# A two-layer diffusion trunk on one core: VectorE takes over GpSimd's parts of h^T and of weights around the ends of sublayers

## The chip, the core and the metric

The kernel runs on one core of one Trainium2 chip, as one launch. The time is the device time of that launch in microseconds, as the median of several runs. The core has five engines that run their own instruction streams in order and meet through semaphores: TensorE (PE, matrix products and transposes), VectorE (DVE), ScalarE (ACT), GpSimd (POOL) and SyncE (SP, which here issues most transfers).

## The reference: what is computed

640 tokens of width 1024 (128 context tokens, then 512 latent ones) go through two layers of three sublayers each: an FFN, a mixer, an FFN. Each sublayer is

```python
h = rms_norm(x, g_norm[i, 0]) * (1.0 + scale) + shift
y, aux = fn(h)
return x + weight * gate * rms_norm(y, g_norm[i, 1]), aux
```

where `shift`, `scale` and `gate` come from a product of the conditioning with `w_mod`, one set for context and one for latent tokens. `fn` is a SwiGLU of inner width 2816 (sublayers s = 0, 2, 3, 5), gated linear attention (GLA) with 4 heads and two scan directions (s = 1), or multi-head latent attention with 16 heads (s = 4). In GLA, q, k, v, an output gate r and a low-rank z are projections of h; the logarithm of the decay is `log_sigmoid(z @ w_gate + b_gate) / 16` for each head and direction; the scan in chunks of 64 tokens yields o, which is normalised, gated by silu(r) and multiplied with `w_out`. All is float32.

## The kernel before

**Tiles and precision.** The tokens are five tiles of 128, in two groups: g = 0 is tiles 0 to 2, g = 1 tiles 3 and 4. h is kept transposed (h^T, eight blocks of 128 features). To keep float32's accuracy with TensorE's faster format, each operand is split into a rounded high part (hi) and the remainder (lo), and each product is three matmuls (`mm3`, L116 to L118: hi by hi, hi by lo, lo by hi). So every weight and every h^T needs a cast on ScalarE (L109, L418, L1054) and a subtraction (L111, L419, L1055) on VectorE or GpSimd. Which of the two takes a weight's lo part is a list, `self.lo`, that rotates with each `split`: it is GpSimd alone during GLA's heads, and GpSimd and VectorE in turn in some of the output projections.

**A sublayer's end.** `sweep` multiplies the inner result with the output weights, tile by tile, and `chain` then takes each tile t through the end of the sublayer and the start of the next: the sum of squares of y on ScalarE (L139), the factors of the norm on VectorE (L126 to L134), the product with the gate (L440), the sum with x (L443), the norm of the new x, the normalisation (L447), eight transposes on TensorE (L406), and the scale and shift as eight activations (L417) into `hraw`, followed by hi (L418) and lo (L419). A store of x goes out on GpSimd's queue (L444). The chain of g = 0 runs beside the products of g = 1. `sum_rows` adds a later modulation row on VectorE during four of the sweeps.

**An FFN's start.** The first two of 22 columns of blocks, f = 0 and 1, are ordinary products. The others use a scheme with seven products of half size instead of eight: `mix` builds three differences of quarters of h^T (`tt`, tiles t1, t2, t3, each hi and lo), and `mixed_weights` four sums of quarters of a weight block (L591 to L594) for each unit u, of which there are 20. For s = 2, 3 and 5 `mix` is called in `chain`, in two pieces: columns 0 to 191 of each half after tile 3, and 192 to 319 after tile 4; its lo parts are GpSimd's. The weights come through three buffers (`raw`), so a load waits until the tile three before it is split.

**GLA.** `gla` loads tables, makes z and the gate weights wg, then for head 0 q and k (`gla_qk`), the logarithms (`gla_log`, `gla_log_end`), their sums (`gla_decay`) and v (`gla_v`). Then for each head h: the weights of head h + 1 are loaded and split, `gla_head` does the scan of head h in seven levels (L1022 to L1033: differences, an exponential, a product with q and k, five matmuls, a masked copy), and the projections and logarithms of head h + 1 follow.

**Order.** The code is written without an explicit order; a scheduler puts it into one stream per engine by priorities that follow the order of the program text and by its own estimates of durations, and within an engine the order is then fixed. `later` gives a part a later priority.

## Time and profile before

| | us |
|---|---|
| median of 3 runs | 2798.01 |
| lowest, highest | 2792.17, 2800.95 |
| the profiled execution | 2802.07 |
| its span in the profile | 2800.3 |

All durations below come from the profiled execution, whose own time is 1.8 us over its span and 4.1 over the median. Its page gives the share of each engine: TensorE 96% of the span, VectorE 68%, ScalarE and GpSimd 48% each, and a mean granted TensorE clock of 0.984. The stages by time: the first FFN to about 505, GLA to about 888, the FFNs of s = 2 and 3 to about 1352 and 1820, latent attention to about 2353, the last FFN to the end. In rows of the timeline the first number is the start, the second the busy time; xN counts instructions in one row, and the bracket at the end gives the idle time of the engine just before the row and what ended it. In the rows of stretches, the counts of instructions stand in brackets behind each engine's busy time. Line numbers are those of the kernel before.

### The profile page before, as it was taken

To read this page: it belongs to the slowest core of one execution; us is meant where nothing else is said; L and a number is where in the kernel's file an instruction comes from. 1 tells how busy PE (TensorE), PEld (TensorE's weight loads), DVE (VectorE), ACT (ScalarE), POOL (GpSimd) and SP (SyncE) were. 2 spreads that over 40 slices of the span, in tenths; PEclk is the share of its full clock that TensorE was granted. 3 is DMA by queue.
4 is the path that set the end of the run, shared out by engine and by line. 5 is a ranking of instruction groups with operands and counts; after the bars stand their busy time and mean duration, and the time that the engine had idled before them with its cause. 6 is when DMAs were issued, how large, how long until landed. Compare 5 with 4: busy or idle time off the path is not lost.

```text
span 2800.3 us, 43895 instructions
## 1 busy us (share of the span) xinstructions
PE 2698.8 (96%) x16670; PEld 2445.7 (87%) x16670; DVE 1896.2 (68%) x2499; ACT 1357.5 (48%) x2460; POOL 1344.8 (48%) x1093
## 2 busy tenths in 40 slices
PE   6999999899998999999999999999999998999998
PEld 5999987788877899987899998789999887999987
DVE  6777666577746767667776756677666677777636
ACT  3544426545546544425544433565555536445423
POOL 2555455343224555555456555404333367556534
PEclk9999999999999999999999999999999999999999
DMA  8444556311225344467344455641111285222445
GB/s 240 145 152 163 183 197 225 115 53 50 65 89 174 106 143 144 158 205 253 124 130 136 132 179 203 208 125 42 47 41 62 77 266 180 69 90 91 165 142 186
DMA packets 227378, 389.03 MB, mean 139 GB/s; under 512 B 17096, under 2 KB 160752, under 8 KB 227168
## 3 DMA queue, kind: packets, MB, share of 16 engines
q1 hardware_dynamic: 217968, 364.16, 40.2%
q0 software_dynamic: 5264, 19.24, 1.8%
q10 hardware_dynamic: 3936, 2.84, 0.4%
q8 instruction: 131, 2.15, 0.3%
q14 instruction: 79, 0.65, 0.1%
HBM read 356.00 MB, written 30.18 MB: 138 GB/s over the span
## 4 chain that ended last, share of the span: by engine, by line
PE 84%; DVE 7%; ACT 2%; DMA 2%; issue 2%; POOL 1%; SPq 0%; ACTq 0%; DVEq 0%; POOLq 0%
PE p L117 9%; PE p L116 9%; PE p L118 9%; PE x L116 7%; PE x L118 7%; PE x L117 7%; PE z L116 3%; PE z L117 3%; PE z L118 3%; PE m L305 2%; PE q L116 2%; PE q L117 2%; PE q L118 2%; PE j L116 2%; PE t L118 2%
## 5 line engine op out<-in xcount | busy, mean ns | idle before, releaser
L109 ACT CAST whi<-raw 128x1024 fp32r<-128x1024 f32 (+1 forms) x288 | 300.0, 1044 | 478.3 <-PE p L118 278.6
L111 DVE TENSOR_TENSOR wlo<-raw,whi 128x1024 fp32r<-128x1024 f32 (+1 forms) x248 | 340.6, 1381 | 262.5 <-ACT whi L109 259.5
L116 PE MATMUL p<-whi,t1h 128*128 128x512 f32 x1040 | 410.6, 395 | 1.9 <-POOL t1h L524 1.2
L118 PE MATMUL p<-whi,t1l 128*128 128x512 f32 x1040 | 408.4, 393 | 1.3 <-POOL t1l L525 1.3
L117 PE MATMUL p<-wlo,t1h 128*128 128x512 f32 x1040 | 408.3, 393 | 0.0
L1055 DVE TENSOR_TENSOR wlo<-raw,whi 128x512 fp32r<-128x512 f32 (+2 forms) x273 | 295.5, 1093 | 132.4 <-ACT whi L1054 131.3
L1055 DVE TENSOR_TENSOR wlo<-s,whi 128x512 fp32r<-128x512 f32 x320 | 280.1, 885 | 91.1 <-PE m L305 51.3
L591 POOL TENSOR_TENSOR s<-raw,raw 128x512 f32<-128x512 f32 x80 | 108.1, 1351 | 441.5 <-DMA raw<-in_w_ffn_in_dram 343.6
L1054 ACT CAST whi<-raw 128x512 fp32r<-128x512 f32 (+2 forms) x273 | 165.3, 610 | 164.3 <-PE q L117 72.0
L1054 ACT CAST whi<-s 128x512 fp32r<-128x512 f32 x320 | 194.3, 618 | 97.1 <-PE z L117 50.0
L116 PEld LDWEIGHTS p<-whi,t1h 128*128 128x128 f32 x1040 | 196.7, 189 | 45.4 <-issue 3.0
L118 PEld LDWEIGHTS p<-whi,t1l 128*128 128x128 f32 x1040 | 196.6, 189 | 43.9 <-POOL t1l L525 2.2
L117 PEld LDWEIGHTS p<-wlo,t1h 128*128 128x128 f32 x1040 | 196.8, 189 | 40.8 <-issue 0.2
L1316 POOL TENSOR_SCALAR p<-p,st 128x640 f32<-128x640 f32 (+1 forms) x68 | 119.9, 1763 | 203.4 <-DVE st L1315 187.8
L116 PE MATMUL x<-hh,whi 128*128 128x320 f32 x640 | 204.1, 319 | 3.5 <-DVE aT L628 3.5
L524 POOL TENSOR_SCALAR t1h<-aT 128x384 fp32r<-128x384 f32 (+1 forms) x128 | 91.9, 719 | 228.5 <-PE p L117 189.0
L118 PE MATMUL x<-hh,wlo 128*128 128x320 f32 x640 | 197.7, 309 | 0.0
L117 PE MATMUL x<-hl,whi 128*128 128x320 f32 x640 | 197.5, 309 | 0.0
L111 POOL TENSOR_TENSOR wlo<-raw,whi 128x1024 fp32r<-128x1024 f32 x40 | 107.2, 2690 | 160.4 <-ACT whi L109 158.7
L525 POOL TENSOR_TENSOR t1l<-aT,t1h 128x384 fp32r<-128x384 f32 (+1 forms) x128 | 143.5, 1122 | 10.0
L116 PEld LDWEIGHTS x<-hh,whi 128*128 128x128 f32 x640 | 120.0, 188 | 28.4 <-issue 24.3
L592 POOL TENSOR_TENSOR s<-s,raw 128x512 f32<-128x512 f32 x80 | 133.7, 1671 | 0.2
(427 smaller groups left out, 7968.0 us busy)
## 6 DMA issues: line engine op xcount, KB each, us to landing
raw<-in_w_ffn_out_dram SPq DMA_DIRECT2D x176, 512.0 KB
raw<-in_w_ffn_in_dram SPq DMA_DIRECT2D x160, 512.0 KB
wm<-in_w_mod_dram SPq DMA_DIRECT2D x112, 512.0 KB
raw<-in_w_mod_dram SPq DMA_DIRECT2D x32, 512.0 KB
raw<-in_mla_w_out_dram SPq DMA_DIRECT2D x32, 512.0 KB
xd<-x POOLq DMA_DIRECT2D x25, 512.0 KB, 3.7
x<-xd SPq DMA_DIRECT2D x25, 512.0 KB
raw<-in_w_ffn_in_dram SPq DMA_DIRECT2D x32, 256.0 KB
```

What stands on the lines that cost most here:

```text
L109: nc.scalar.copy(hi[:, :n], src[:, :n])
L111: (self.lo[0]).tensor_tensor(lo[:, :n], src[:, :n], hi[:, :n].bitcast(F32), op=ALU.subtract)
L116: mm(out, lh, rh, start=start, stop=False, **kw)
L117: mm(out, lh, rl, start=False, stop=False, **kw)
L118: mm(out, ll, rh, start=False, stop=stop, **kw)
L524: self.nc.gpsimd.tensor_scalar(ah, a, 1.0, 0.0, op0=ALU.mult, op1=ALU.add)
L525: self.nc.gpsimd.tensor_tensor(al, a, ah.bitcast(F32), op=ALU.subtract)
L591: G(s1, w21, w22, op=ALU.add)
L592: G(s2, s1, w11, op=ALU.subtract)
L1054: self.nc.scalar.copy(hi, src)
L1055: (engine or self.nc.vector).tensor_tensor(lo, src, hi.bitcast(F32), op=ALU.subtract)
L1316: (nc.gpsimd if h < MH - 1 else V).tensor_scalar(pp, pp, ri, None, op0=ALU.mult)
```

## The change

What it does, in five parts:

1. `sum_rows` issues the small loads and memsets of a row (`mod_gains`) ahead of its first load of weights, and `sweep` takes this first step at its start.
2. The lo part of h^T is always VectorE's (`gentle` is gone), and the mix of h^T is made in one piece after tile 4, with all its operations on VectorE and each difference split as soon as it is there.
3. The sums for unit 0's weights are VectorE's in the FFNs of s = 2, 3 and 5; the other units' sums stay GpSimd's.
4. All of GLA's lo parts (head weights, wg, output projection) are VectorE's.
5. In GLA, z's weights get two tiles of the pool `room` instead of the common weight buffers; wg is split after z's first product; v of the first group comes before z's second product; the masks are loaded by SP, later; and each head's logarithms are made one head earlier.

```diff
 def sum_rows(self, ps):
         for p in ps:
             o = (p % 9) * D
+            b = self.mod_gains(p)
+            yield
             acc = [...]
...
-                if kc == 0:
-                    b = self.mod_gains(p)
 def to_hT(...):
-        (nc.gpsimd if gentle else nc.vector).tensor_tensor(
-            hT[1][:, :, c : c + P], h, hT[0][:, :, c : c + P].bitcast(F32), op=ALU.subtract
-        )
+        nc.vector.tensor_tensor(hT[1][:, :, c : c + P], h, hT[0][:, :, c : c + P].bitcast(F32), op=ALU.subtract)
 def chain(...):
-                self.to_hT(u, hT, t, g, pt, cols=cols[:, :, cond, :], raw=raw, gentle=s == 2 and g == 0)
-                if ffn and t > 2:
-                    self.mix(slice(0, 4), *((0, 192), (192, HT))[t - 3], nc.gpsimd)
+                self.to_hT(u, hT, t, g, pt, cols=cols[:, :, cond, :], raw=raw)
+        if g and s in (2, 3, 5):
+            self.mix(slice(0, 4), 0, HT)
 def sweep(...):
+        next(steps, None)
-    def mix(self, ks, a, b, engine=None):
+    def mix(self, ks, a, b):
+        split = lambda t, src: self.hi_lo(t[0][:, ks, a:b], t[1][:, ks, a:b], src)
         V.tensor_tensor(h11, h12, h11, op=sub)
+        split(self.tt[0], h11)
         V.tensor_tensor(h12, h22, h12, op=sub)
         V.tensor_tensor(h22, h22, h11, op=sub)
+        split(self.tt[1], h22)
         V.tensor_tensor(h21, h21, h22, op=sub)
-        for t, src in zip(self.tt, (h11, h22, h12)):
-            self.hi_lo(t[0][:, ks, a:b], t[1][:, ks, a:b], src, engine)
+        split(self.tt[2], h12)
 def mixed_weights(..., engine):
-        G = nc.gpsimd.tensor_tensor
+        G = engine.tensor_tensor
 def ffn(...):
-            W[u] = self.mixed_weights(w_in, u % 2, f)
+            W[u] = self.mixed_weights(w_in, u % 2, f, nc.gpsimd if u or s == 0 else V)
 def gla(...):
-            mf = self.scratch(896).rearrange("p (l i) -> p l i", i=P)
-            nc.scalar.dma_start(mf, I["masks"])
-            nc.vector.tensor_copy(masks, mf)
-            nc.vector.tensor_scalar(diag2, self.ident, 2.0, None, op0=ALU.mult)
-            wz = [self.wp.tile([P, 1024], F32R, tag=x, ...) for x in ("whi", "wlo")]
+            wz = [T_([P, 1280], "room", F32R, bufs=7)[...] for _ in range(2)]
...
-            nc.scalar.copy(wg, wv)
-            nc.sync.dma_start(wv[97:98], wg[96:97].bitcast(F32))
-            nc.gpsimd.tensor_tensor(wg[64:], wv[64:], wg[64:].bitcast(F32), op=ALU.subtract)
             self.gla_z(0, hT, wz, z)
+            nc.scalar.copy(wg, wv)
+            nc.sync.dma_start(wv[97:98], wg[96:97].bitcast(F32))
+            nc.vector.tensor_tensor(wg[64:], wv[64:], wg[64:].bitcast(F32), op=ALU.subtract)
             low = [self.gla_log(0, 0, z, wg, o_all, "a")]
             self.gla_qk(0, hT, head, True)
+            self.gla_v(0, hT, head, nc.vector.tensor_copy)
             self.gla_z(1, hT, wz, z)
...
-            for g in range(2):
-                self.gla_v(g, hT, head, nc.vector.tensor_copy)
+            logs = lambda h: self.gla_log_end(h, o_all, [self.gla_log(h, g, z, wg, o_all, "d") for g in range(2)])
+            self.gla_v(1, hT, head, nc.vector.tensor_copy)
+            logs(1)
+            mf = self.scratch(896).rearrange("p (l i) -> p l i", i=P)
+            nc.sync.dma_start(mf, I["masks"])
+            nc.vector.tensor_copy(masks, mf)
+            nc.vector.tensor_scalar(diag2, self.ident, 2.0, None, op0=ALU.mult)
             for h in range(GH):
...
-                    self.gla_log_end(h + 1, o_all, [self.gla_log(h + 1, g, z, wg, o_all, "d") for g in range(2)])
                     for g in range(2):
                         self.gla_qk(g, hT, nxt)
                         if g == 0:
                             b = self.gla_decay(room, o_all, tri, h + 1)
+                            if h + 2 < GH:
+                                logs(h + 2)
...
-            lo, self.lo = self.lo, [nc.vector]
...
-        self.lo = lo
...
-            if g:
-                self.lo = [nc.gpsimd, nc.vector]
 def run(self):
-                self.lo = [self.nc.gpsimd]
```

How the order of instructions moves, at three places. The first is VectorE at the start of the FFN of s = 2, from tile 4's normalisation (`t_1079`, in the change `t_1073`) on; `aT_7525` holds h^T in `hraw`, `s_...` are the sums of unit 0's weights out of its two loads. A line of the kernel before is up to two lower or higher in the change (L447 is L445, L591 is L592, L594 is L595). Before:

```order
L447 TENSOR_SCALAR t_1069_7996<-x_7994,st_7997 128x1024
L130 SCALAR_TENSOR_TENSOR st_8052<-st_8052 128x1
L134 SCALAR_TENSOR_TENSOR st_8052<-st_8052 128x1
L447 TENSOR_SCALAR t_1079_8051<-x_8049,st_8052 128x1024
L560 TENSOR_TENSOR aT_7525<-aT_7525 128x4x192
L419 TENSOR_TENSOR hl<-aT_7525,hh 128x8x128
L561 TENSOR_TENSOR aT_7525<-aT_7525 128x4x192
L560 TENSOR_TENSOR aT_7525<-aT_7525 128x4x128
```

After:

```order
L445 TENSOR_SCALAR t_1069_7996<-x_7994,st_7997 128x1024
L130 SCALAR_TENSOR_TENSOR st_8036<-st_8036 128x1
L592 TENSOR_TENSOR s_8353<-raw_8349,raw_8351 128x512
L134 SCALAR_TENSOR_TENSOR st_8036<-st_8036 128x1
L595 TENSOR_TENSOR s_8354<-raw_8349 128x512
L445 TENSOR_SCALAR t_1073_8035<-x_8033,st_8036 128x1024
L593 TENSOR_TENSOR s_8353<-s_8353,raw_8349 128x512
L594 TENSOR_TENSOR s_8354<-raw_8351,s_8353 128x512
L419 TENSOR_TENSOR hl<-aT_7525,hh 128x8x128
L560 TENSOR_TENSOR aT_7525<-aT_7525 128x4x320
```

Two of the four sums now stand ahead of tile 4's normalisation, the first of them with both loads of unit 0 as its inputs, and the mix follows both tiles' lo parts in one width of 320 per half.

The second is GpSimd at the same place: the last rows of the chain (`xd` is the stored x), then what follows. Before:

```order
L419 TENSOR_TENSOR hl<-aT_7525,hh 128x8x128
L444 DMA xd_110<-x_7994 128x1024
L444 DMA xd_110<-x_8049 128x1024
L591 TENSOR_TENSOR s_8363<-raw_8359,raw_8361 128x512
L594 TENSOR_TENSOR s_8364<-raw_8359 128x512
L592 TENSOR_TENSOR s_8363<-s_8363,raw_8359 128x512
L593 TENSOR_TENSOR s_8364<-raw_8361,s_8363 128x512
L1055 TENSOR_TENSOR t1l_8034<-aT_7525,t1h_8033 128x4x192
L1055 TENSOR_TENSOR t3l_8038<-aT_7525,t3h_8037 128x4x192
```

After:

```order
L442 DMA xd_110<-x_7725 128x1024
L442 DMA xd_110<-x_7770 128x1024
L442 DMA xd_110<-x_7809 128x1024
L442 DMA xd_110<-x_7994 128x1024
L442 DMA xd_110<-x_8033 128x1024
L592 TENSOR_TENSOR s_8497<-raw_8493,raw_8495 128x512
L593 TENSOR_TENSOR s_8497<-s_8497,raw_8493 128x512
```

Between the five stores nothing is left, and its first sums are those of unit 1.

The third is ScalarE in head 0: the activation of a level (L1027), the copy of kdm (L991) that the products with the states wait for, the absolute value, exponential and logarithm of the next logarithms (L902, L910, L911), and the projections (L872). Before, with the logarithms of head 1:

```order
L1027 ACTIVATE t_719_5535<-t_719_5535 128x1280
L1012 COPY H_5505<-a_711_5495 128x256
L902 ACTIVATE o_all_5022<-d_746_5653 128x2x256
L910 ACTIVATE o_all_5022<-o_all_5022 128x5x256
L1012 COPY H_5518<-a_714_5508 128x256
L911 ACT_TABLE_LOAD
L911 ACTIVATE o_all_5022<-o_all_5022 128x5x256
L872 ACTIVATE room_5640<-j_747_5662 128x384
L1027 ACT_TABLE_LOAD
L1027 ACTIVATE t_721_5549<-t_721_5549 128x1280
```

After, the same logarithms of head 1, now ahead of kdm:

```order
L902 ACTIVATE o_all_5018<-d_693_5427 128x2x256
L910 ACTIVATE o_all_5018<-o_all_5018 128x5x256
L911 ACT_TABLE_LOAD
L911 ACTIVATE o_all_5018<-o_all_5018 128x5x256
L872 ACTIVATE room_5660<-j_747_5662 128x384
L991 COPY kdm_643_5021<-a_714_5499 64x640
L991 COPY kdm_642_5020<-a_715_5507 64x640
L872 ACTIVATE room_5660<-j_748_5688 128x384
L1027 ACT_TABLE_LOAD
L1027 ACTIVATE t_722_5541<-t_722_5541 128x1280
```

The logarithms left the middle of the levels for a place ahead of kdm and of the first level after it; those of head 2 follow later in the same head.

## The prediction

> **What bounds the kernel now.** I read the page first: engines, chain, and the two groups of weight lo parts.

> ```profile
> PE 2698.8 (96%) x16670; PEld 2445.7 (87%) x16670; DVE 1896.2 (68%) x2499; ACT 1357.5 (48%) x2460; POOL 1344.8 (48%) x1093
> PE 84%; DVE 7%; ACT 2%; DMA 2%; issue 2%; POOL 1%; SPq 0%; ACTq 0%; DVEq 0%; POOLq 0%
> L111 DVE TENSOR_TENSOR wlo<-raw,whi 128x1024 fp32r<-128x1024 f32 (+1 forms) x248 | 340.6, 1381 | 262.5 <-ACT whi L109 259.5
> L111 POOL TENSOR_TENSOR wlo<-raw,whi 128x1024 fp32r<-128x1024 f32 x40 | 107.2, 2690 | 160.4 <-ACT whi L109 158.7
> ```

> TensorE is the bound, and its work does not change: only its idle time (the span of 2800.3 less 2698.8, 101.5 us) and its slow clock can be won. So next the PE timeline: every matmul that begins after a wait in the places that the change touches. The bracket holds the wait and who ended it.

> ```profile
> 347.13 0.47 PE L116 MATMUL p<-whi,t1h 128*128 128x512 f32 x1 [0.78 <-DVE bm L358]
> 519.69 0.66 PE L406 MATMUL p<-ident,t 128*128 128x128 f32 x2 [5.17 <-DVE st L127]
> 584.04 1.35 PE L1032 MATMUL a<-t 128*128 128x128 f32 x10 [1.47 <-DVE t L1028]
> 626.51 0.67 PE L1005 MATMUL a<-room,kdm 128*128 128x256 f32 x2 [2.58 <-DVE kdm L991]
> 820.95 1.09 PE L406 MATMUL a<-ident,o_all 128*128 128x128 f32 x8 [3.13 <-DVE t L410]
> 862.86 1.69 PE L406 MATMUL p<-ident,t 128*128 128x128 f32 x8 [1.85 <-DVE t L447]
> 873.08 1.63 PE L406 MATMUL p<-ident,t 128*128 128x128 f32 x8 [2.49 <-DVE st L127]
> 889.08 0.44 PE L117 MATMUL p<-hl,whi 128*128 128x384 f32 x1 [1.20 <-POOL hl L419]
> 912.57 0.79 PE L116 MATMUL p<-hh,whi 128*128 128x256 f32 x2 [4.99 <-ACT hh L418]
> 915.33 0.58 PE L117 MATMUL p<-hl,whi 128*128 128x256 f32 x1 [1.97 <-DVE hl L419]
> 1362.61 1.07 PE L406 MATMUL p<-ident,t 128*128 128x128 f32 x8 [2.30 <-DVE st L128]
> 1377.97 0.39 PE L117 MATMUL p<-hl,whi 128*128 128x256 f32 x1 [1.99 <-DVE hl L419]
> 2379.00 0.58 PE L117 MATMUL p<-hl,whi 128*128 128x256 f32 x1 [2.27 <-DVE hl L419]
> 2397.40 0.42 PE L116 MATMUL x<-hh,whi 128*128 128x320 f32 x1 [3.45 <-DVE aT L628]
> ```

> Nearly all wait for VectorE at a sublayer's end or a head. GLA's start and heads by stretches:

> ```profile
> 505.00:562.00 57.00, 45.81 (x308) 43.75 (x307) 33.35 (x51) 33.51 (x54) 20.54 (x12) 0.88 0.37 108
> 562.00:622.00 60.00, 56.55 (x408) 53.27 (x406) 43.97 (x58) 32.65 (x52) 24.90 (x20) 1.00 0.15 45
> 622.00:681.00 59.00, 54.21 (x374) 50.71 (x373) 42.76 (x54) 30.64 (x51) 23.02 (x19) 0.97 0.15 45
> 681.00:740.00 59.00, 53.60 (x370) 50.55 (x370) 43.05 (x56) 30.05 (x49) 12.76 (x15) 0.97 0.29 90
> ```

> The columns are the stretch's length, busy time of PE, weight loads, VectorE, ScalarE and GpSimd, granted clock, DMA share and GB/s. PE is idle 11.2 us in GLA's start and 3.5 + 4.8 + 5.4 = 13.7 in three heads.

> Why VectorE is late shows on the VectorE and GpSimd timelines side by side:

> ```profile
> 514.05 5.49 DVE L447 TENSOR_SCALAR t<-x,st 128x1024 f32<-128x1024 f32 x1
> 514.34 4.64 POOL L111 TENSOR_TENSOR wlo<-raw,whi 128x1024 fp32r<-128x1024 f32 x2
> 862.80 3.61 DVE L111 TENSOR_TENSOR wlo<-raw,whi 128x1024 fp32r<-128x1024 f32 x1
> 862.95 2.37 POOL L111 TENSOR_TENSOR wlo<-raw,whi 128x1024 fp32r<-128x1024 f32 x1
> 885.57 1.23 DVE L111 TENSOR_TENSOR wlo<-raw,whi 128x1024 fp32r<-128x1024 f32 x1 [2.96 <-ACT whi L109]
> 897.21 0.75 DVE L447 TENSOR_SCALAR t<-x,st 128x1024 f32<-128x1024 f32 x1
> 815.78 3.98 DVE L811 SCALAR_TENSOR_TENSOR o_all<-o_all,r,room 128x256 f32<-128x256 f32 x2 [4.10 <-ACT room L808]
> 812.24 9.74 POOL L111 TENSOR_TENSOR wlo<-raw,whi 128x1024 fp32r<-128x1024 f32 x4 [50.48 <-ACT whi L109]
> ```

> The normalisation takes 0.75 us alone and 5.49 beside two GpSimd lo parts; a lo part 1.23 alone and 3.61 beside one that takes 2.37. So a GpSimd operation costs VectorE about its whole length (1.23 + 2.37 = 3.60). On VectorE the same piece costs 1.23. That is the gain to be had: each moved lo part takes about 1.2 us out of the way of whatever VectorE does beside it, and leaves GpSimd quiet. [...]

> A second price is the clock after a wait:

> ```profile
> 584.00:586.00 2.00, 1.96 (x17) 1.00 0.00 0
> 864.00:866.00 2.00, 2.00 (x7) 0.50 0.95 270
> 866.00:868.00 2.00, 2.00 (x9) 0.85 1.01 412
> ```

> After the 1.47 us wait the granted clock stays 1.00; after the 1.85 us wait it is 0.50 for about three us, which costs 1.0 + 0.3 and a little ahead, 1.5 us. I add 1.5 to each removed wait of 1.85 us or more, save the 3.45 one, where I take the wait alone. [...]

> **The change, part by part.**

> *First values early.* The gains' memsets and small loads come before the first raw load: the 0.78 wait goes. Gain 0.7 (bounds 0 to 0.8; eight small DMAs go ahead of one 512 KB load on SP, at a time when the sweep has six chunks of slack). The other three sweeps show no such wait: nothing.

> *GLA's start.* The lo parts of heads 0 and 1 and of wg leave GpSimd. Tile 3's normalisation is 0.75 instead of 5.49, so the 5.17 wait ends some 2 to 3 us sooner, and tile 4's with it. Against it, the z weight's lo part now stands on VectorE behind tile 3's chain, two more raw loads wait for splits, and the masks' load moves to SP with VectorE waiting for it. Clock lost now: at most 45.81 x 0.12 = 5.5, about 4. Of 15 us at stake I take 5 (bounds -2 to 10): what VectorE frees at once (5.49 - 0.75), no more.

> *Heads.* Four lo parts per head go from GpSimd to VectorE: 4 x 1.23 = 4.9 us more on VectorE, whose 43 us of 59 include about as much stretching by them. The logarithms of head h+2 come a head earlier, after the decay, so the wait of 1.47 for the levels behind the table loads goes in heads 1 and 2 (2.9), and the two waits of 2.58 for kdm shrink to about 1.2 without the clock loss (2 x 1.4 + 2 x 1.5 = 5.8). Head 0 now carries two sets of logarithms and VectorE gets fuller: minus 2.7 (one wait like 2.58). Gain 6 (bounds -3 to 11, where 11 leaves out this loss and adds smaller waits).

> *Output projection and FFN start behind GLA.* The 3.13 wait stood behind two gating steps of 3.98 beside four GpSimd lo parts: it goes, 3.0 + 1.5 = 4.5. The waits 1.85, 2.49 and 1.20 go but for 0.8 of the second: 1.85 + 1.5 + 1.7 + 1.5 + 1.2 = 7.8. For the 4.99 and 1.97, the mix in one piece lets ScalarE cast tile 4's h^T before the mix's parts, and no GpSimd runs. But a new wait comes, from the sums of unit 0:

> ```profile
> 893.31 2.87 SPq L580 DMA_DIRECT2D raw<-in_w_ffn_in_dram  x2
> 899.64 1.29 POOL L591 TENSOR_TENSOR s<-raw,raw 128x512 f32<-128x512 f32 x1 [4.33 <-issue]
> 905.48 2.80 POOL L1055 TENSOR_TENSOR t1l<-aT,t1h 128x768 fp32r<-128x768 f32 x1
> 921.88 0.68 DVE L1055 TENSOR_TENSOR wlo<-s,whi 128x512 fp32r<-128x512 f32 x1
> 1355.44 1.63 POOL L591 TENSOR_TENSOR s<-raw,raw 128x512 f32<-128x512 f32 x1 [10.37 <-DMA raw<-in_w_ffn_in_dram]
> L963 DVE TENSOR_TENSOR room<-room,room x4: 1482/1491/1491, 554.0 to 729.0; 128x1280 f32<-128x1280 f32 x4
> ```

> The second raw tile of unit 0 is issued at 893.31 and the sums begin at 899.64, after tile 4's normalisation at 897.21. In the new order two sums stand ahead of that normalisation on VectorE, so it waits for this load and then for 2 x 0.68: tile 4's transposes come some 4 us later than now against the group's end. I count a new wait of 5 plus 1.5 of clock in place of 4.99 + 1.97 + 2 x 1.5: gain 3.5, and 0.5 off for VectorE's fuller queue. Part: 4.5 + 7.8 + 3 = 15.3 (bounds 6 to 21).

> *FFN start of s=3.* The load has landed at 1355.44, before VectorE comes to the sums; four sums (2.7 us) stand between the normalisations of tiles 3 and 4, but no GpSimd stretches them: the 2.30 wait falls by about 1, without clock loss in one of two cases: 1. The 1.99 goes (3.5). Gain 4.5 (bounds 1 to 6).

> *FFN start of s=5.* At the transposes nothing; the 2.27 goes with its clock (3.8), of the 3.45 about 2.2, since the last product of the first units stands on VectorE ahead of h^T's own lo part now. Gain 6 (bounds 2 to 9).

> *The mix and sums as work.* Each FFN start gives VectorE three lo parts of 128x1280 (nearest row 1.49) and four sums (nearest 0.68): 4.5 + 2.7 = 7.2 us, three times 21.6, in place of GpSimd's pieces (2.80 for the larger). I cost it at nothing more: it lies beside the products of f = 0 and 1 for tiles 3 and 4, which need none of it. Without that cover it is 21.6.

> Sum: 0.7 + 5 + 6 + 15.3 + 4.5 + 6 = 37.5, off the profiled execution's 2802.07: 2764.6. That execution is 4.1 above the median of 2798.01; the same off the median gives 2760.5, and I give 2761.

> **Rivals.** (a) *The moved work takes the place of the stretching*: the 21.6 us above stand in VectorE's in-order queue ahead of what PE waits for. For it: VectorE is already 73% busy in the heads (43 of 59). Against it: PE comes back to these operands only after the other group's products. 37.5 - 21.6 = 16: 2782. (b) *VectorE becomes the bound*, slower: 28 GLA lo parts x 1.23 = 34.4 and the 21.6 make 56; if all of it fell on the path, 56 - 37.5 = 18.5 slower, 2816. It turns slower once two thirds of the 56 (37.5) fall there. Against it: PE's 13.7 us of idle in the heads leave VectorE 16 us a head. (c) *The stretching is not GpSimd's*: the long VectorE operations also stand beside transfers (DMA share 0.95 to 1.01 in 864 to 868). Then the waits stay and shift: 2798. Against it: 1.23 + 2.37 fits 3.61 so closely. (d) *More comes back*: all waits named go with their clock, about 55 instead of 37.5: 2743.

> **How the numbers follow.** This kernel's runs tell about 0.3% (8.4 us) from no change. Forecast 0.58 (gain 25 to 48, 2750 to 2773); (a) 0.22, all of it faster still; (b) 0.07; (c) 0.06; (d) 0.07. Range 2744 to 2790: it leaves out (b), (c) and the end of (d). Faster 0.87, same 0.06, slower 0.07.

> **What would show it.** Right: normalisations at 0.75 and lo parts at 1.23 at every sublayer's end; no wait of PE for tile 3's transposes near 515 over 4 us, nor near 820 over 1; the clock at 1.00 there. In the FFN start behind GLA one wait of 3 to 6 us for tile 4's transposes, behind a sum that waits for its raw load: if it is missing, the gain is some 6 us larger. Wrong: waits in the heads for VectorE's kdm or levels longer than 2.58, or a wait of PE for z in GLA's start over 4 us.

## The result, and the profile after

| | before | changed |
|---|---|---|
| median, us | 2797.01 (4 runs) | 2759.97 (4 runs) |
| lowest to highest | 2792.17 to 2800.95 | 2757.02 to 2763.89 |
| profiled execution | 2802.07 | 2758.97 |

The ratio is 0.9862 (95% interval 0.9843 to 0.9881): 37 us by the medians, where 2761 had been forecast. The profiled executions lie 43.1 apart, since that of before is a slow draw, 5.1 over its median, and that of the changed kernel 1.0 under.

The page of the changed kernel, engines, chain and lo parts of weights, in the lines that answer to those of before:

```profile
PE 2678.3 (97%) x16670; PEld 2425.4 (88%) x16670; DVE 1884.9 (68%) x2540; ACT 1354.7 (49%) x2451; POOL 1202.4 (44%) x1031
PE 84%; DVE 6%; ACT 4%; DMA 3%; issue 2%; POOL 1%; SPq 0%; ACTq 0%; DVEq 0%; POOLq 0%
L111 DVE TENSOR_TENSOR wlo<-raw,whi 128x1024 fp32r<-128x1024 f32 (+1 forms) x276 | 375.7, 1368 | 259.6 <-ACT whi L109 256.0
```

VectorE has 41 instructions more and is busy 11 us less; GpSimd lost 142 us. TensorE does the same 16670 matmuls in 20.5 us less (the clock), and idles 78.9 us (2757.2 - 2678.3) instead of 101.5. So of the 43.1 about half is waits and half is clock; the mean granted clock rose from 0.984 to 0.995.

The changed kernel's PE timeline, the matmuls after the waits that the prediction spoke of (the bracket is the wait):

```profile
347.34 0.47 PE L116 MATMUL p<-whi,t1h 128*128 128x512 f32 x1 [0.78 <-DVE bm L358]
590.49 2.48 PE L1032 MATMUL a<-t 128*128 128x128 f32 x10 [2.16 <-DVE t L1028]
857.11 1.07 PE L406 MATMUL p<-ident,t 128*128 128x128 f32 x8 [2.12 <-DVE st L128]
881.71 1.09 PE L406 MATMUL p<-ident,t 128*128 128x128 f32 x8 [2.29 <-DVE t L445]
890.74 0.39 PE L117 MATMUL p<-hl,whi 128*128 128x256 f32 x1 [0.75 <-DVE hl L419]
1337.78 1.06 PE L406 MATMUL p<-ident,t 128*128 128x128 f32 x8 [1.31 <-DVE t L445]
1346.78 0.39 PE L117 MATMUL p<-hl,whi 128*128 128x256 f32 x1 [0.76 <-DVE hl L419]
2326.40 1.07 PE L406 MATMUL p<-ident,t 128*128 128x128 f32 x8 [1.83 <-DVE st L128]
2338.19 0.39 PE L117 MATMUL p<-hl,whi 128*128 128x256 f32 x1 [0.76 <-DVE hl L419]
2353.15 0.42 PE L118 MATMUL q<-hh,wlo 128*128 128x320 f32 x1 [3.12 <-DVE wlo L1055]
```

The 5.17 us at GLA's start, the 3.13 at the output projection and the 4.99 at the FFN start behind GLA are gone; a wait of 2.29 for tile 4's transposes stands there now, and in the last FFN one of 3.12, for a weight's lo part, where one of 3.45 stood. VectorE, in the same places:

```profile
516.96 0.75 DVE L445 TENSOR_SCALAR t<-x,st 128x1024 f32<-128x1024 f32 x1
846.76 1.22 DVE L111 TENSOR_TENSOR wlo<-raw,whi 128x1024 fp32r<-128x1024 f32 x1
879.63 0.69 DVE L592 TENSOR_TENSOR s<-raw,raw 128x512 f32<-128x512 f32 x1 [2.45 <-issue]
```

The normalisation that took 5.49 takes 0.75, the lo part that took 3.61 takes 1.22, and the first sum waits 2.45 us with tile 4's normalisation behind it, as foretold. The row names no releaser; the second load of unit 0 was issued at 873.51, 6.1 us ahead of the sum, as it was 6.3 us ahead of GpSimd's first sum in the kernel before (893.31 and 899.64).

Marks on PE, the same matmul in both profiled executions, show where the time went (starts in us; the last two columns are the difference and what the stage added to it):

| mark | before | changed | ahead by | stage |
|---|---|---|---|---|
| head 0, first scan product (L972) | 562.04 | 554.16 | 7.9 | 7.9 |
| head 3, the same | 736.30 | 724.48 | 11.8 | 3.9 |
| first transpose of o | 801.10 | 789.51 | 11.6 | -0.2 |
| tile 0 of h^T for s = 2 | 862.86 | 844.42 | 18.4 | 6.8 |
| s = 2, first unit's product | 929.28 | 902.11 | 27.2 | 8.7 |
| tile 0 of h^T for s = 3 | 1311.00 | 1283.99 | 27.0 | -0.2 |
| s = 3, first unit's product | 1390.84 | 1358.16 | 32.7 | 5.7 |
| tile 0 of h^T for s = 4 | 1770.47 | 1736.36 | 34.1 | 1.4 |
| tile 3 of h^T for s = 5 | 2363.57 | 2326.40 | 37.2 | 3.1 |
| s = 5, last unit's product | 2642.2 | 2599.2 | 43.0 | 5.8 |

### The profile page after: what moved, and what is told of

The parts are those of the page before. It is cut to its first block, busy times and chain, and to the rows that moved or that the text cites. A ratio compares the mean times of both kernels' runs of the same rounds, so it can differ in the third digit from the quotient of the medians.

```text
span 2757.2 us, 43843 instructions
## 1 busy us (share of the span) xinstructions
PE 2678.3 (97%) x16670; PEld 2425.4 (88%) x16670; DVE 1884.9 (68%) x2540; ACT 1354.7 (49%) x2451; POOL 1202.4 (44%) x1031
## 4 chain that ended last, share of the span: by engine, by line
PE 84%; DVE 6%; ACT 4%; DMA 3%; issue 2%; POOL 1%; SPq 0%; ACTq 0%; DVEq 0%; POOLq 0%
PE p L116 8%; PE p L117 8%; PE p L118 8%; PE x L116 7%; PE x L118 7%; PE x L117 7%; PE z L116 3%; PE z L118 3%; PE z L117 3%; PE m L305 2%; PE q L118 2%; PE q L116 2%; PE q L117 2%; PE t L118 2%; PE t L116 2%
## 5 line engine op out<-in xcount | busy, mean ns | idle before, releaser
L111 DVE TENSOR_TENSOR wlo<-raw,whi 128x1024 fp32r<-128x1024 f32 (+1 forms) x276 | 375.7, 1368 | 259.6 <-ACT whi L109 256.0
L109 ACT CAST whi<-raw 128x1024 fp32r<-128x1024 f32 (+1 forms) x288 | 300.1, 1044 | 468.4 <-PE p L118 252.6
L116 PE MATMUL p<-whi,t1h 128*128 128x512 f32 x1040 | 409.4, 394 | 2.1 <-POOL t1h L523 1.2
L117 PE MATMUL p<-wlo,t1h 128*128 128x512 f32 x1040 | 407.4, 392 | 0.0
L1055 DVE TENSOR_TENSOR wlo<-raw,whi 128x512 fp32r<-128x512 f32 (+1 forms) x272 | 292.5, 1086 | 131.5 <-ACT whi L1054 130.6
L1055 DVE TENSOR_TENSOR wlo<-s,whi 128x512 fp32r<-128x512 f32 x320 | 281.1, 891 | 83.9 <-PE m L305 47.6
L592 POOL TENSOR_TENSOR s<-raw,raw 128x512 f32<-128x512 f32 x77 | 107.2, 1392 | 473.4 <-DMA raw<-in_w_ffn_in_dram 389.7
L1054 ACT CAST whi<-raw 128x512 fp32r<-128x512 f32 (+1 forms) x272 | 164.5, 609 | 166.3 <-PE q L117 72.0
L116 PEld LDWEIGHTS p<-whi,t1h 128*128 128x128 f32 x1040 | 196.1, 189 | 45.5 <-issue 2.8
L117 PEld LDWEIGHTS p<-wlo,t1h 128*128 128x128 f32 x1040 | 195.9, 188 | 40.6 <-issue 0.2
L116 PE MATMUL x<-hh,whi 128*128 128x320 f32 x640 | 204.2, 319 | 0.0
L117 PE MATMUL x<-hl,whi 128*128 128x320 f32 x640 | 197.7, 309 | 0.0
L116 PEld LDWEIGHTS x<-hh,whi 128*128 128x128 f32 x640 | 120.1, 188 | 24.7 <-issue 24.3
L593 POOL TENSOR_TENSOR s<-s,raw 128x512 f32<-128x512 f32 x77 | 126.8, 1646 | 0.2
L595 POOL TENSOR_TENSOR s<-raw 128x512 f32<-128x512 f32 x77 | 123.8, 1608 | 0.0
```

Of the source, the lines that this page charges most:

```text
L109: nc.scalar.copy(hi[:, :n], src[:, :n])
L111: (self.lo[0]).tensor_tensor(lo[:, :n], src[:, :n], hi[:, :n].bitcast(F32), op=ALU.subtract)
L116: mm(out, lh, rh, start=start, stop=False, **kw)
L117: mm(out, lh, rl, start=False, stop=False, **kw)
L592: G(s1, w21, w22, op=ALU.add)
L593: G(s2, s1, w11, op=ALU.subtract)
```

## Experiments

Two theories stood against each other. The prediction's: an operation of GpSimd (there a lo part, which reads two tiles) costs VectorE about its whole length (3.61 us against 1.23 beside one of 2.37), so GpSimd's parts cost more time than VectorE's would. The rival: it is the lateness of the parts on a slow engine, or the new order of the work, that made the difference. Medians of the changed kernel for comparison: 2759.97 at first and 2758.05 once more, on the chip of two of the runs (VectorE's useless work, and latent attention's output weights). The kernel before ran beside each set of runs, with medians of 2797.01, 2794.79, 2794.74 and 2798.72; so 2 or 3 us between kernels of different sets tell nothing.

**GpSimd reads for nothing.** Beside each of the 16 splits of GLA's head weights (the new operation is on `nc.gpsimd`; `self.extra` is set for these splits alone):

```diff
+            wide = lambda x: x[:, :P].unsqueeze(1).to_broadcast([P, 8, P])
+            nc.gpsimd.tensor_tensor(self.extra[0], wide(self.ident), wide(hi.bitcast(F32)), op=ALU.subtract)
         return hi, lo
```

> The changed kernel, with one more GpSimd operation beside each split of GLA's head weights (16 of them): it subtracts 128 columns of the split's high part from the identity, both read eight times over (128x1024), and writes a tile that nobody reads. VectorE still makes the lo parts, nothing waits for the new operations, and no load or product hangs on them. Theory (GpSimd's reads stop VectorE): VectorE's normalisation near 515 and the products of the levels are stretched by 1 to 2.4 us where they meet, and of the 11.8 us won from GLA's start to the last head, 6 to 10 are lost: 2766 to 2770 us. Rival (what cost time before was that the lo parts themselves were late on a slow engine, 2.4 instead of 1.2 us): no change, 2758 to 2762.

Measured: 2784.8, 25 us slower (ratio to before 0.9969, 0.9957 to 0.9981). In the groups of instructions of 505 to 745 us, VectorE's lo parts of the changed kernel (first line) and of this run (second), and the new operations:

```profile
L111 DVE TENSOR_TENSOR wlo<-raw,whi 128x1024 fp32r<-128x1024 f32 x20 | 24.3, 1218 | 4.3 <-ACT whi L109 4.2
```
```profile
L111 DVE TENSOR_TENSOR wlo<-raw,whi 128x1024 fp32r<-128x1024 f32 x18 | 37.4, 2082 | 2.3 <-ACT whi L109 2.2
L114 POOL TENSOR_TENSOR junk<-ident,whi 128x1024 f32<-128x1024 f32 x16 | 47.9, 2996 | 55.6 <-ACT whi L109 55.4
```

And one place of this run's VectorE, GpSimd and PE timelines (L963 is the first product of the decays with k, 1.48 us alone):

```profile
684.16 3.63 DVE L963 TENSOR_TENSOR t<-t,room 128x1280 f32<-128x1280 f32 x1
683.46 6.54 POOL L114 TENSOR_TENSOR junk<-ident,whi 128x1024 f32<-128x1024 f32 x2 [0.31 <-ACT whi L109]
687.85 2.50 PE L981 MATMUL a<-room,t 128*128 128x128 f32 x10 [3.20 <-DVE t L963]
```

VectorE's rows from the end of the first FFN to the first transpose of o, in the changed kernel and in this run (length, VectorE's busy time, clock, DMA share, GB/s):

```profile
505.48:789.51 284.03, 202.48 (x293) 0.99 0.24 73
```
```profile
503.43:812.65 309.22, 232.74 (x293) 0.96 0.22 67
```

A piece of work that nobody waits for costs 25 us: the theory stands, and the rival of late parts falls, for the lo parts stayed VectorE's. So does the rival of the new order, for this loss: between 500 and 800 us VectorE's and ScalarE's instructions stand in the same order as in the changed kernel. The size was wrong, 6 to 10 had been expected: 48 us of GpSimd's reading made the same 293 VectorE instructions 30 us longer, and the stretch 25; TensorE's busy time takes 8 of these (274.9 us instead of 266.9), which is the clock.

**GpSimd writes for nothing.** The same places, but one column read and two clearings in place of the subtraction:

```diff
+            nc.gpsimd.tensor_tensor(junk[:, 0, :1], self.ident[:, :1], hi[:, :1].bitcast(F32), op=ALU.subtract)
+            for _ in range(2):
+                nc.gpsimd.memset(junk, 0.0)
```

> The changed kernel, with GpSimd work beside each split of GLA's head weights as in the run with reading operations, but writing alone: one subtraction of one column, which waits for the split's cast, and then two clearings of a tile of 128x1024 that nobody reads (2.4 us in all by the 0.31 of a clearing of 128x256). Theory that reading is what stops VectorE (its two inputs out of SBUF): no stretching of subtractions, 0 to 4 us slower, 2760 to 2764. Rival, any GpSimd operation stops it: as with the reading operations, some 22 to 25 us slower, 2782 to 2785.

Measured: 2758.25, no change. The same groups of this run:

```profile
L111 DVE TENSOR_TENSOR wlo<-raw,whi 128x1024 fp32r<-128x1024 f32 x19 | 23.1, 1218 | 4.2 <-ACT whi L109 4.1
L116 POOL MEMSET junk<- 128x1024 f32 x30 | 29.1, 969 | 1.7
```

29 us of clearing beside them leave VectorE's lo parts at 1218 ns, and the order of VectorE's and ScalarE's instructions is again that of the changed kernel. What stops VectorE's lo parts is GpSimd's reading, not its running: 2082 ns in the run with the subtractions, 1218 in the run with the clearings. The two runs show it for operations of two inputs. The one normalisation (a single tile as its input) that meets the clearings, at 515, takes 0.93 us instead of 0.75, and the two clearings 2.39 together, where two alone take 1.97 (at 502.85):

```profile
515.41 0.93 DVE L450 TENSOR_SCALAR t<-x,st 128x1024 f32<-128x1024 f32 x1
514.84 2.39 POOL L116 MEMSET junk<- 128x1024 f32 x2
```

**The same useless work on VectorE.**

```diff
-            nc.gpsimd.tensor_tensor(self.extra[0], wide(self.ident), ...)
+            nc.vector.tensor_tensor(self.extra[0], wide(self.ident), ...)
```

> The changed kernel, with the useless subtraction beside each split of GLA's head weights (128x1024, both inputs from SBUF) on VectorE instead of GpSimd: 16 x 1.22 = 19.5 us more for VectorE. It prices the slack of VectorE in GLA, which rival (b) of the prediction lacked. If VectorE has slack (16 us a head by the busy times of before), most is hidden: 0 to 6 us slower, 2760 to 2766. If VectorE sets the pace there: 14 to 20 slower, 2774 to 2780. The same operations on GpSimd cost 25.

Measured: 2765.23, 7 us slower than the changed kernel on the same chip. Of 20.0 us (16 operations) a third comes through: VectorE in GLA is neither free nor the bound. This is the price of rival (b), and the same subtraction costs three to four times as much on GpSimd. It is a rough price: here the scheduler also put VectorE's instructions into another order.

**GLA's lo parts back to GpSimd**, in the changed kernel:

```diff
+                self.lo = [self.nc.gpsimd]
                 hT = self.gla(s, hT)
...
+            lo, self.lo = self.lo, [nc.vector]
...
+        self.lo = lo
...
+            if g:
+                self.lo = [nc.gpsimd, nc.vector]
```

> The changed kernel, with all lo parts of weights in GLA made by GpSimd as in the kernel before (28 of them; wg's stays on VectorE, and so does the new order of z, v and the logarithms). Theory: GpSimd's reading operations stop VectorE for their length. Then the normalisations and level products beside them are stretched again, and of the 27 us that were won up to the first unit of the FFN of s = 2, some 12 to 18 are lost: 2772 to 2778 us. The part that stays is from h^T's lo parts and the mix, which are still VectorE's. Rival, the gain in GLA came from the new order (logarithms a head earlier, z and masks moved): at most 4 us slower, 2760 to 2764.

Measured: 2783.38, 23 us slower (ratio to before 0.9959, 0.9945 to 0.9974), more than expected. By the marks the stretch from the first FFN's last product to the first transpose of o is 305.8 us, against 284.0 in the changed kernel and 296.3 before: with GpSimd's lo parts the new order is worse than the old by 9. Some of VectorE's instructions also change places, so the 23 are not the lo parts' alone.

**GLA's lo parts to VectorE**, in the kernel before, and nothing else:

```diff
-                self.lo = [self.nc.gpsimd]
-            lo, self.lo = self.lo, [nc.vector]
-        self.lo = lo
-            if g:
-                self.lo = [nc.gpsimd, nc.vector]
-            nc.gpsimd.tensor_tensor(wg[64:], ...)
+            nc.vector.tensor_tensor(wg[64:], ...)
```

> The kernel before, with nothing changed but GLA's lo parts (28 weights' and wg's) on VectorE instead of GpSimd. Theory (GpSimd's reads stop VectorE): the stretched normalisation at 514 (5.49 us), the gating step at 816 and the level products go back to their lengths alone; GLA up to the first unit of the FFN of s = 2 wins 12 to 20 of the 27 us, the kernel 12 to 20: 2775 to 2785 where the kernel before has 2795. Rival (the new order of z, v, masks and logarithms is what lets VectorE carry the lo parts): under 6 us won, since VectorE makes the lo parts ahead of what TensorE waits for.

Measured: 2786.18, a gain of 8.6 by the medians (ratio 0.9974, 0.9959 to 0.9989), below the expectation. By the marks, counted from the first FFN's last product, 10.9 are won up to the first unit of s = 2, 2.7 of them up to the first transpose of o. GLA's start, up to head 0's first scan product, wins 5.6 of the changed kernel's 8.6. From there to head 3's first scan product this run needs 177.1 us, where the kernel before needs 174.3 and the changed one 170.3. So in the heads VectorE's lo parts alone win nothing; they need the new order too.

**The logarithms in their own head again**, in the changed kernel:

```diff
-            logs(1)
...
+                    logs(h + 1)
                     for g in range(2):
                         self.gla_qk(g, hT, nxt)
                         if g == 0:
                             b = self.gla_decay(room, o_all, tri, h + 1)
-                            if h + 2 < GH:
-                                logs(h + 2)
```

> The changed kernel, with each head's logarithms made where the kernel before makes them (those of head h + 1 after head h's scan). Theory of the prediction: the waits for the level products behind the exponential and the logarithm come back in heads 0 to 2, about 1.5 to 2 us each, and the two sets that head 0 carries now (a wait of 2.16 us at 588) and the logarithms ahead of head 0's first product (about 2 us of GLA's start) go: 1 to 4 us slower, 2761 to 2764. Rival: head 0's double load costs as much as the later heads win: the same within 1 us, or up to 3 faster.

Measured: 2762.95, 3 slower than the changed kernel by the medians, as expected, but within its spread of runs. By the marks the same stretch to the first transpose of o is 288.4 against 284.0: head 0's first scan product comes 0.5 us sooner, and the heads take 4.9 more.

**The mix in two pieces with GpSimd's lo parts**, in the changed kernel (`mix` itself as before):

```diff
-        if g and s in (2, 3, 5):
-            self.mix(slice(0, 4), 0, HT)
+                if ffn and t > 2:
+                    self.mix(slice(0, 4), *((0, 192), (192, HT))[t - 3], nc.gpsimd)
```

> The changed kernel, with the mix of h^T in two pieces and its lo parts on GpSimd, as before; the sums of unit 0 and all else stay on VectorE. Theory: GpSimd's six lo parts (1.5 to 2.8 us) stretch VectorE's lo part of tile 4 and the mix itself, and ScalarE's cast of tile 4 comes behind casts of the first piece: each of the three FFN starts loses 3 to 5 us, together 9 to 15: 2769 to 2775 us. Rival (a): the 4.5 us of lo parts that VectorE has in each FFN start cost as much as they save: the same within 3 us.

Measured: 2770.79, 11 slower. Its PE timeline at the FFN start of s = 2 has two waits again where the changed kernel has one of 0.75:

```profile
888.97 0.50 PE L116 MATMUL p<-hh,whi 128*128 128x256 f32 x2 [1.95 <-ACT hh L418]
892.39 0.58 PE L117 MATMUL p<-hl,whi 128*128 128x256 f32 x1 [2.92 <-DVE hl L419]
```

VectorE and GpSimd just ahead of the second:

```profile
889.52 2.82 DVE L419 TENSOR_TENSOR hl<-aT,hh 128x1024 fp32r<-128x1024 f32 x1
888.73 2.52 POOL L1053 TENSOR_TENSOR t2l<-aT,t2h 128x768 fp32r<-128x768 f32 x1
```

The same pair of waits stands in s = 3 and s = 5. Rival (a), that the 4.5 us of lo parts cost VectorE as much as they save, falls. But the run puts back two things at once. The second wait is for the most part GpSimd's reading: tile 4's lo part takes 2.82 us beside it, and 1.22 in the changed kernel. The first is the two pieces: ScalarE casts three parts of the first piece (0.83 to 0.84 us each) ahead of tile 4's h^T. No run prices the two apart.

**Unit 0's sums back to GpSimd, and unit 1's to VectorE**, each alone in the changed kernel (the two added lines are the two runs):

```diff
-            W[u] = self.mixed_weights(w_in, u % 2, f, nc.gpsimd if u or s == 0 else V)
+            W[u] = self.mixed_weights(w_in, u % 2, f, nc.gpsimd)
+            W[u] = self.mixed_weights(w_in, u % 2, f, nc.gpsimd if u > 1 or s == 0 else V)
```

> The changed kernel, with the four sums of unit 0 back on GpSimd in all FFNs. Prediction's working: in s = 2 the wait of tile 4's transposes for a sum that waits for its load (2.29 us) goes, in s = 3 and 5 GpSimd's sums stretch the normalisation of tile 3 or 4 and the product with gates by 1 to 1.5 us each. Together within 2 us of the changed kernel: 2758 to 2762. Theory of GpSimd's stops alone, without that wait: 3 to 5 slower, 2763 to 2766.

> The changed kernel, with the sums of unit 1 on VectorE too in the FFNs of s = 2, 3 and 5. Theory: in s = 5 the splits of unit 0's weights that stand beside GpSimd's sums of unit 1 (2.4 and 1.7 us instead of 0.69) go back to 0.69, and the wait of 3.12 us of TensorE at 2350 falls to 1 or less: 2 to 3 us faster, 2757 to 2758. Rival: 2.7 us more work on VectorE ahead of the same splits, and its waiting for unit 1's load, cost as much: the same or 1 to 3 slower.

Measured: 2759.27 and 2752.62. The first is no change, as expected: the wait for tile 4 in s = 2 goes, and others come (tile 3's in s = 3 is 2.30 instead of 1.31 for tile 4). So this part of the change brings nothing by itself. The second is 5 to 7 us faster by the medians (its four runs lie from 2752.1 to 2755.9, nine of the changed kernel from 2755.6 to 2763.9), but only 2 by the ratio to before (0.9854, 0.9837 to 0.9871, against 0.9862 and 0.9860 for the changed kernel): its size is open. In the changed kernel VectorE's splits of unit 0 in s = 5 had stood beside GpSimd's sums of unit 1:

```profile
2349.06 2.37 DVE L1055 TENSOR_TENSOR wlo<-s,whi 128x512 fp32r<-128x512 f32 x2
2351.36 1.74 DVE L1055 TENSOR_TENSOR wlo<-raw,whi 128x512 fp32r<-128x512 f32 x1
```
```profile
2347.29 1.30 POOL L592 TENSOR_TENSOR s<-raw,raw 128x512 f32<-128x512 f32 x1 [22.04 <-DMA raw<-in_w_ffn_in_dram]
2348.66 1.61 POOL L593 TENSOR_TENSOR s<-s,raw 128x512 f32<-128x512 f32 x1
2350.96 1.59 POOL L594 TENSOR_TENSOR s<-raw,s 128x512 f32<-128x512 f32 x1 [0.69 <-DVE wlo L1055]
```

VectorE's two rows hold three splits, 4.1 us where three alone take 2.0 (0.68 each), and TensorE's wait of 3.12 us behind them is 0.54 in the second run.

**Latent attention's output weights too.** On top of the last, `self.lo = [nc.vector]` for both groups there, where eight lo parts of g = 1 are GpSimd's in turn.

> The changed kernel, with the sums of unit 1 on VectorE (as in the run that was 7 us faster) and with all lo parts of latent attention's output weights on VectorE too (eight of them are GpSimd's in turn). Theory: GpSimd's lo parts there (2.4 to 3.4 us) stretch VectorE's small factors of the norm (2.16 us instead of 0.2 at 2295) and the normalisation (1.31 instead of 0.75), and delay the t1 parts that GpSimd itself makes for TensorE (waits of 0.93 and 1.16); the waits of 2.31 and 0.77 us at the transposes there fall by half: 2 to 5 us faster than with the sums alone, 2748 to 2751. Rival: VectorE is then late with the weights, or GpSimd's t1 parts still stop it: the same as with the sums alone, 2752 to 2755.

> The changed kernel once more, on the same chip as the next two, as their measure: 2757 to 2763 us, by its runs so far (2757.0 to 2763.9).

Measured on one chip: 2753.60 and, for the changed kernel, 2758.05; so both steps together win 4.5 us. Beyond the sums the second brings nothing that can be told: 2752.62 had been measured without it. GpSimd goes on making the t1 parts there, and reads as it does so.

## Why the prediction was right

*The mechanism* held as it was read from pairs of rows: a GpSimd operation that reads costs a VectorE one beside it up to about its own length (2.37 us made 3.61 out of 1.23 in the kernel before). Reading without use shows it (+25), writing without use bounds it (0). Rival (c), transfers, falls with the same pair of runs, since the loads are the same. Rival (b) was priced too high: a third of added VectorE work in GLA comes through. Rivals (a) and (d) fall by the time, 37 us won instead of 16 or 55.

*The sum*, step by step: the forecast, of it what was counted for the clock, and the same by the marks (there the clock is what TensorE's busy time became shorter):

| step | forecast | of it clock | marks | of it clock |
|---|---|---|---|---|
| first FFN (first values early) | 0.7 | 0 | -0.7 | 0.2 |
| GLA's start | 5 | 0 | 8.6 | 2.7 |
| heads | 6 | 3 | 3.7 | 1.4 |
| output projection, FFN start of s = 2 | 15.3 | 6 | 15.6 | 7.6 |
| FFN start of s = 3 | 4.5 | 1.5 | 5.7 | 2.8 |
| FFN start of s = 5 | 6 | 1.5 | 5.8 | 4.0 |
| the stages between | 0 | 0 | 4.4 | 1.8 |

Most of the last row is not the change's: with the code of before in latent attention, the run with VectorE's lo parts in GLA alone takes 590.0 us from tile 0 for s = 4 to tile 3 for s = 5, as the changed kernel does (590.0); the profiled execution of before took 593.1. Without that row, 38.7 stand against 37.5.

*First values early* was mis-read. The wait of 0.78 stands unchanged at 347.34. What TensorE waits for there is VectorE's addition of the bias to the row (`mod_store`, L358), which reads the row's sums (`m`) in PSUM; the product's row names it as its releaser (`bm`). The loads of that bias had never been late. Just ahead of the addition VectorE makes a lo part that takes 2.28 us beside a GpSimd product of 1.57, in both kernels: at 1.22 it would have ended 1.06 sooner, more than the wait (an estimate from these rows). The mechanism was right here too, but the change left this pair in place.

*GLA's start* was put at 5, what VectorE frees at once, and gave 5.9 of waits and 2.7 of clock, for which nothing had been counted. *Heads* were put at 6 and gave 3.7: head 0's doubled logarithms cost a wait of 2.16 in its levels (590.49), as allowed for, but VectorE's lo parts by themselves gave nothing there (177.1 us against 174.3).

*FFN start of s = 5* is right in its sum alone. Of the 3.45, 2.2 had been taken to go; the 3.12 that stands there now, behind weights' lo parts beside GpSimd's sums, leaves 0.3. Waits gave 1.8 instead of 4.5, the clock 4.0 instead of 1.5.

*The new wait* of tile 4 came by the mechanism foretold, a sum in VectorE's queue that waits for its load, but 2.3 us long, not 5, and without clock loss. It hangs on the loads of that run: in the second run of the changed kernel it is 2.18, in the run with two units' sums on VectorE 0.49.

*The clock* was mis-sized. I credited 1.5 us to each removed wait of 1.85 us or more, 12 in all; 20.5 came, not all of it at these places. And length does not decide alone. In every trace of this case half clock lasts 3.41 us, or two or three times that (the end of the program aside; it lasts 10.24 at 515.03 and 910.98 in the kernel before), and its starts lie whole steps of 3.413 us (10.24 / 3) apart: in the changed kernel at 463.99, 590.29 and 2300.36, 37 and 501 steps. Cut into these steps, the wait of 1.85 us in the kernel before (columns: length, PE busy, clock, DMA share, GB/s):

```profile
859.78:863.19 3.41, 1.56 (x9) 1.00 0.37 137
863.19:866.60 3.41, 3.41 (x13) 0.50 0.93 267
```

And the waits of 2.16, 2.29 and 3.12 of the changed kernel:

```profile
586.88:590.29 3.41, 1.45 (x13) 1.00 0.01 2
590.29:593.70 3.41, 3.21 (x15) 0.50 0.00 0
877.01:880.42 3.41, 2.41 (x17) 1.00 1.02 356
880.42:883.83 3.41, 2.12 (x15) 1.00 0.11 37
883.83:887.25 3.42, 3.42 (x22) 1.00 0.00 0
2348.15:2351.56 3.41, 1.88 (x16) 1.00 0.00 0
2351.56:2354.98 3.42, 1.83 (x12) 1.00 0.00 0
2354.98:2358.39 3.41, 3.41 (x25) 1.00 0.50 150
```

*Lucky or right?* The sum is within 2 us of the medians, but three terms (GLA's start, heads, first values) were off by 1 to 4 us each and cancelled. And the waits gave 20.0 where 25.5 were forecast, the clock 18.7 where 12 were (without the last row), at the FFN start of s = 5 above all. The mechanism was right; that the number is as close as this is in part luck.

## What to carry to other kernels

Look for VectorE operations whose duration varies in the timeline, and lay GpSimd's rows beside them: if the excess is the length of a GpSimd operation that reads (here 3.61 us against 1.23, beside one of 2.37), moving that piece to VectorE can shorten the chain although VectorE gets more to do. Clearings could stay on GpSimd here where VectorE's operations beside them read two tiles (lo parts of 1218 ns with them and without). Before moving, ask what stands behind each moved operation in VectorE's fixed order, above all behind one that waits for a load, and which GpSimd reader is next to run beside the same chain: here the next unit's sums, which were worth another 2 to 7 us. Judge a wait not by its length alone, but by how much idle time falls into one step of the clock with it (here steps of 3.41 us, and 1.5 us idle or more in each that half clock followed).

## What was not expected of the hardware

That 48 us of GpSimd reading which nobody waits for cost a kernel of 2758 us 25 us, while 29 us of GpSimd clearing at the same places cost nothing. And that a TensorE wait of 3.12 us can leave the granted clock at 1.00 where one of 1.85 us had halved it: the first lay across the end of a step of 3.41 us, with no more than 1.6 us idle on either side, and the second within one step.
